# A hybrid diffusion block on one core: r feature-major, s and the output projection in 512-column pieces

## Chip, core and metric

The kernel runs on one core of one Trainium2 chip. The metric is the device time of one execution in microseconds (us). TensorE (PE) multiplies, with its weight load (PEld) beside it; VectorE (DVE), ScalarE (ACT) and GpSimd (POOL) do the element work; SyncE (SP) issues most transfers from a queue in order. The chip grants TensorE one of two clock levels, 1.2 or 2.4 GHz; 1.00 in the profile is the higher one.

## The reference

One layer over 1024 tokens of width 1024, with 256 context tokens, all in fp32. What matters here is the token mixer:

```python
z_a, q, k, v, r, lr_f, lr_b, gates = split_cols(h @ w_in)      # one input projection; z_a = (u, s)
y_a = spatial_gating(gelu(z_a), ...) @ w_a                     # u * (128x128 mixing of layer_norm(s))
o   = gla forward + gla backward                               # gated linear attention, 4 heads, both directions
o_n = o * rsqrt(mean(o * o) + EPS) * gla_g                     # per head
y_b = (o_n * silu(r)) @ w_b
x   = x + gt1 * ((g_a * y_a + g_b * y_b) @ w_out)
```

After it the x is normalised again, a router picks two of sixteen experts for each token, and the experts' feed-forward is added. The kernel spends the second half of its time on the experts, which the change does not touch.

## The kernel before

Every fp32 matrix is split in two parts, a high part rounded to the type that TensorE multiplies fast (`wh`, `hxh`) and the rest (`wl`, `hxl`). A product is three matmuls: high by high, high by low, low by high (`gemm`, L251 to L256). A contraction over 1024 has 8 steps of 128, so a gemm of one tile is 24 matmuls. A weight chunk of 1 MB is loaded by SP (`wraw`, two buffers), rounded by ScalarE (L236, 128x2048) and subtracted by VectorE (L237); `wh` and `wl` have two buffers each. The normalised input stays on the chip with features on the partitions (`H`).

The stages, in order of time: v and the low-rank gates; k and q; **r** (268 to 360 us); the GLA over the context (to 413 us) and over the tokens, first half (to 543 us) and second half (to 688 us); **s** (to 779 us); position mixing with ga (to 870 us); the projections w_a and w_b (to 1036 us); the **output projection** with residual, norm and router (to 1150 us); the experts.

- r (L583 to L594): four chunks of 256 output columns. For each of eight token tiles the tokens are stationary and the 256 weight columns move. ScalarE applies silu out of PSUM (L593), SP stores to `r_d`, token by token. k (L573 to L581) has it the other way: 128 weight columns stationary, 512 tokens moving, one full PSUM bank.
- GLA (L776 to L808): eight pairs of blocks of 128 tokens, one forward and one backward. From the fifth pair on a block has been seen by the other direction: `op` (the other direction's output) and `rb` (its rows of r) are loaded, VectorE adds, normalises by head and multiplies by r (L801, four instructions). After each pair come two side tiles, 48 matmuls each, that make gb, u or ga (`side_tile`); behind each side tile one second block is transposed on TensorE (tile `ogt`, L759), scaled by `gla_g` on ScalarE (L762, eight instructions of 128x128) and stored (`turned_out`).
- A block itself (`gla_block`): VectorE makes `ke` (L656); TensorE transposes it (`keT`); ScalarE and VectorE split it (`kt0` L661, `kt1` L662); attention, masked by VectorE (L677), split again; `o` and `s` tiles of matmuls; VectorE updates the states (L699).
- s (L823 to L830): four chunks of 256 columns, tokens stationary, as r; gelu by ScalarE (L829), statistics of 256 columns by VectorE (L830).
- Output projection (L986 to L1012, loop at L1202): w_out in four pieces of 256 columns, two in the shared buffers and two in their own. A token tile has two halves of 512 columns, each in one PSUM bank and made of two pieces. VectorE multiplies a half by gt1 (L1010) and adds x (`xt`, L1011); TensorE transposes the tile (L1023) for the router, and VectorE has its many small operations of 16 columns and fewer, for the tile before, between the two halves.

A recording layer and a scheduler write each engine's instructions in an order; each engine then runs its own list strictly in order. `issue_after` holds a piece of work in that order behind a given instruction.

Of the kernel before, what the change touches and what calls it, by code (L numbers as in the profile page):

```python
# [6 lines left out]
F32 = mybir.dt.float32  # L7
# [11 lines left out]
S = 1024  # L19
# [43 lines left out]
            + [("s", 1024 + 256 * i, 256) for i in range(4)]  # L63
# [58 lines left out]
def lay_out(x, c, ctx, c_ctx, w_mod, b_mod, g_norm1, g_norm2, w_in, w_gate2, b_gate2, gla_norm_g, sgu_ln_g,  # L122
# [28 lines left out]
    A["w_out"] = tiled(np.asarray(w_out)[0], 8, 256)  # L151
# [9 lines left out]
def body(tc, A, out):  # L161
# [15 lines left out]
    r_d = scratch((S, D), "r_d")  # L177
# [405 lines left out]
    for j in range(4):  # L583
        w = w_in("r", j)
        if j == FOLD:
            fold_router()
        if j < 2:
            mod_chunk(6 + j)
        for i in range(8):
            p = mm()  # L590
            gemm(p[:, :256], H(128 * i, 128), W_(w, 0, 256), 8)
            s = tv.tile([128, 264], F32, name="vs", bufs=3)
            silu_end = SC.activation(s[:, :256], p[:, :256], AF.Silu)  # L593
            SP.dma_start(r_d[128 * i:128 * i + 128, 256 * j:256 * j + 256], s[:, :256])  # L594
# [159 lines left out]

    def turned_out(b, ob, gt):
        for h in range(2):
# [3 lines left out]
            for k in range(4):  # L760
                c = 4 * h + k
                SC.activation(gt[:, 128 * c:128 * c + 128], p[:, 128 * k:128 * k + 128], AF.Copy,  # L762
                              scale=cols[:, C_GLA + c:C_GLA + c + 1])
        SP.dma_start(gT_d[b], gt)

    seen = set()
    for i in range(8):
        for d in range(2):
# [10 lines left out]
            if second:  # L779
                op = t1.tile([128, D], F32, name="op", bufs=2)  # L780
                SP.dma_start(op, o_d[t0:t0 + 128])
                rb = t1.tile([128, D], F32, name="rb", bufs=1)
                SP.dma_start(rb, r_d[t0:t0 + 128])
# [15 lines left out]
            for h in range(4):  # L799
                hs = slice(256 * h, 256 * h + 256)  # L800
                V.scalar_tensor_tensor(ob[:, hs], ob[:, hs], ss[:, 4 + h:5 + h], rb[:, hs],  # L801
                                       op0=ALU.mult, op1=ALU.mult)
            late.append((b, ob, gt))
        for n in range(SIDE[i]):
# [17 lines left out]
    bst = [t1.tile([128, 4, 6], F32, name=f"bst{i}") for i in range(8)]  # L822
    for j in range(4):  # L823
        w = w_in("s", j)
        for i in range(8):
            p = mm()
            gemm(p[:, :256], H(128 * i, 128), W_(w, 0, 256), 8)
            s = vs[i][:, 256 * j:256 * j + 256]
            SC.activation(s, p[:, :256], AF.Gelu_apprx_tanh)  # L829
# [9 lines left out]
    t1.release()  # L839
    zp = tc.alloc_tile_pool(name="zp", bufs=1, side="right", reuse_waits="tile")  # L840
# [109 lines left out]
    for j in range(4):  # L950
        raw = wp.tile([128, WMAX], F32, name="wraw", tag="wraw", bufs=2)
        SP.dma_start(raw[:, :2048], A["w_out"][j])
        if j < 2:
            wo.append(split(raw, 2048, 8, wp))
        else:
            wh = t1.tile([128, 8, 256], F32R, name=f"woh{j}")
            wl = t1.tile([128, 8, 256], F32R, name=f"wol{j}")
# [754 lines left out]
```

## Time and profile before

| | us |
|---|---|
| median of 3 runs | 2205.27 |
| lowest, highest | 2201.27, 2208.33 |
| the profiled execution's own time | 2202.61 |
| its span in the profile | 2200.9 |
| TensorE busy | 2146.6 (98%) |
| VectorE busy | 1413.5 (64%) |
| ScalarE busy | 1054.0 (48%) |

The span is what the records cover; 1.7 us of the execution's time lie around it. A stage's window shows how long the stage takes and how much of it each engine is busy; the timeline gives start, duration, engine and line of each instruction, and in brackets how long its engine had been idle and for what.

### The profile page before, as it was taken

Reading aid. Unit: us, or ns where it says so; the run is one execution under the profiler, and the core shown is the slowest. Engines: PE = TensorE matmul, PEld = TensorE weight load, DVE = VectorE, ACT = ScalarE, POOL = GpSimd, SP = SyncE. Lnnn points to the kernel's source line nnn. Section 1 sums busy time; section 2 is a strip of 40 time slices with the busy share of each in tenths; the row PEclk is TensorE's granted clock in tenths of the full one; section 3 lists DMA queues with packets and bytes.
Section 4 is the critical chain, followed back from the end, with each engine's and each line's share of the span. In section 5 each row is a group of like instructions: output and inputs, shape, how many; then the busy total and the mean of one; then the engine's idle time right before and its main releaser. Section 6 shows DMA issues by size and latency. Waiting matters only on the chain. (4 is left out here: it accounts for less than half of the span.)

```text
span 2200.9 us, 36059 instructions
## 1 busy us (share of the span) xinstructions
PE 2146.6 (98%) x14288; PEld 1786.6 (81%) x14289; DVE 1413.5 (64%) x2123; ACT 1054.0 (48%) x1327; POOL 201.7 (9%) x172
## 2 busy tenths in 40 slices
PE   8999999999999999999996999999999999999996
PEld 6999898888889987888995777787878777777774
DVE  5654213856763244435788778787878787786766
ACT  3412113644543134323225566676757666665653
POOL 0011000000000000000231301010101010101021
PEclk9999999999999999999997999999999999999998
DMA  7576443465662155644566989798989889897764
GB/s 301 178 221 178 158 145 112 163 201 182 204 232 80 46 205 198 219 151 147 183 248 225 340 298 369 305 371 298 378 305 352 327 325 349 303 366 289 278 235 171
DMA packets 142031, 530.20 MB, mean 241 GB/s; under 512 B 17210, under 2 KB 57842, under 8 KB 94752
## 3 DMA queue, kind: packets, MB, share of 16 engines
q1 hardware_dynamic: 119920, 468.03, 57.8%
q0 software_dynamic: 20784, 55.54, 8.6%
q10 hardware_dynamic: 1152, 4.26, 0.6%
q8 instruction: 114, 1.87, 0.3%
q14 instruction: 61, 0.50, 0.1%
HBM read 457.55 MB, written 70.31 MB: 240 GB/s over the span
## 5 line engine op out<-in xcount | busy, mean ns | idle before, releaser
L1192 DVE TENSOR_TENSOR hl<-praw,hl 128x2048 fp32r<-128x2048 f32 x173 | 395.8, 2291 | 119.9 <-ACT hl L1191 114.5
L1372 PE MATMUL pa<-hl,xah 128*128 128x512 f32 x1536 | 418.7, 394 | 2.0 <-DVE hl L1192 1.0
L1191 ACT ACTIVATE hl<-praw 128x2048 fp32r<-128x2048 f32 x173 | 331.9, 1919 | 146.5 <-PE pa L1372 146.5
L1372 PEld LDWEIGHTS pa<-hl,xah 128*128 128x128 f32 x1536 | 285.9, 189 | 65.6 <-DVE hl L1192 4.3
L1192 DVE TENSOR_TENSOR hl<-raw,hl 128x2048 fp32r<-128x2048 f32 x115 | 263.1, 2291 | 86.3 <-ACT hl L1191 82.5
L1191 ACT ACTIVATE hl<-raw 128x2048 fp32r<-128x2048 f32 x115 | 220.7, 1919 | 105.2 <-PE pa L1372 100.4
L1372 PE MATMUL pa<-hl,xal 128*128 128x512 f32 x768 | 237.3, 390 | 0.0
L255 PE MATMUL mm<-wh,hxh 128*128 128x256 f32 (+1 forms) x768 | 219.3, 286 | 0.7 <-DVE ctx_v L284 0.4
L255 PE MATMUL mm<-wl,hxh 128*128 128x256 f32 (+1 forms) x768 | 218.0, 284 | 0.0
L255 PE MATMUL mm<-wh,hxl 128*128 128x256 f32 (+1 forms) x768 | 217.7, 284 | 0.0
L1372 PE MATMUL pa<-hl,aah 128*128 128x512 f32 x768 | 211.7, 397 | 0.0
L255 PE MATMUL mm<-hxh,wh 128*128 128x512 f32 x448 | 176.7, 394 | 0.0
L255 PE MATMUL mm<-hxh,wl 128*128 128x512 f32 x448 | 176.5, 394 | 0.0
L255 PE MATMUL mm<-hxl,wh 128*128 128x512 f32 x448 | 176.5, 394 | 0.0
L1372 PEld LDWEIGHTS pa<-hl,xal 128*128 128x128 f32 x768 | 144.6, 188 | 30.8
L1372 PEld LDWEIGHTS pa<-hl,aah 128*128 128x128 f32 x768 | 142.1, 189 | 28.2 <-issue 0.4
L255 PEld LDWEIGHTS mm<-wh,hxh 128*128 128x128 f32 x768 | 146.7, 191 | 1.5 <-DVE ctx_v L284 0.6
L255 PEld LDWEIGHTS mm<-wl,hxh 128*128 128x128 f32 x768 | 146.8, 191 | 0.0
L255 PEld LDWEIGHTS mm<-wh,hxl 128*128 128x128 f32 x768 | 146.5, 191 | 0.0
L237 DVE TENSOR_TENSOR wl<-wraw,wh 128x2048 fp32r<-128x2048 f32 (+1 forms) x36 | 82.7, 2298 | 99.0 <-ACT wh L236 78.3
L1372 PE MATMUL pa<-hl,aal 128*128 128x512 f32 x384 | 120.0, 392 | 0.0
L236 ACT ACTIVATE wh<-wraw 128x2048 fp32r<-128x2048 f32 (+1 forms) x36 | 69.0, 1918 | 65.0 <-PE mm L255 64.9
(496 smaller groups left out, 3576.0 us busy)
## 6 DMA issues: line engine op xcount, KB each, us to landing
praw<-in_w_gu_dram SPq DMA_DIRECT2D x114, 1024.0 KB
raw<-in_w_gu_dram SPq DMA_DIRECT2D x78, 1024.0 KB
praw<-in_w_d_dram SPq DMA_DIRECT2D x59, 1024.0 KB
raw<-in_w_d_dram SPq DMA_DIRECT2D x37, 1024.0 KB
wraw<-in_w_in_dram SPq DMA_DIRECT2D x24, 1024.0 KB
wraw<-in_w_mod_dram SPq DMA_DIRECT2D x18, 1024.0 KB
vb<-v_d POOLq DMA_DIRECT2D x16, 1024.0 KB, 6.7
xt<-in_x_dram SPq DMA_DIRECT2D x16, 512.0 KB
```

Of the source, the lines that this page charges most:

```text
L236: SC.activation(wh[:, :n], raw[:, :n], AF.Copy)
L237: V.tensor_sub(wl[:, :n], raw[:, :n], wh[:, :n].bitcast(F32))
L255: end = PE.matmul(acc, Wst[a](k), Wmv[b](k), start=n == 0, stop=n == tot - 1)
L1191: SC.activation(hl[:, 0, :], raw, AF.Copy)
L1192: V.tensor_sub(hl[:, 1, :], raw, hl[:, 0, :].bitcast(F32))
L1372: end = PE.matmul(acc[h], st[x][:, k0 + k, :], w[:, k, 512 * h:512 * h + 512], start=start and (k, n) == (0, 0), stop=stop and (k, n) == ( ...
```

## The change

1. r becomes feature-major: 128 weight columns stationary, 512 tokens moving, 16 tiles in place of 32, and `r_d` has features first.
2. So r can be multiplied only after the transposition. The four multiplies of L801 become four scaled copies on ScalarE, without r, and `turned_out` has VectorE multiply the transposed PSUM tile by `gla_g` and by `rb` in one instruction (eight of 128x128). `rb` has one buffer, is fetched by `gate_b` for the first waiting block, and for the next one as soon as `turned_out` is through with this one.
3. s has two chunks of 512 columns. A chunk's weights are two halves of the contraction (4 steps each). The first chunk's lie in the common `wh`/`wl` buffers, the second's in a new pool `ws` of four tiles.
4. w_out is laid out as four pieces of 512 columns and half the contraction; a tile's half is 24 matmuls of 512 columns in place of 48 of 256.
5. The x rows of a token tile are fetched one tile ahead.

```diff
--- before.py
+++ after.py
@@ -60,7 +60,7 @@
             + [("r", 4096 + 256 * i, 256) for i in range(4)]
             + [("gb", 6176 + 256 * i, 256) for i in range(4)]
             + [("u", 256 * i, 256) for i in range(4)]
-            + [("s", 1024 + 256 * i, 256) for i in range(4)]
+            + [("s", 1024 + 512 * i, 512) for i in range(2)]
             + [("ga", 5152 + 256 * i, 256) for i in range(4)])
 
 
@@ -148,7 +148,7 @@
     A["sgu_w"] = f(np.asarray(sgu_w)[0].transpose(2, 0, 1))
     A["w_a"] = tiled(np.asarray(w_branch_a)[0], 8, 256)
     A["w_b"] = tiled(np.asarray(w_branch_b)[0], 8, 256)
-    A["w_out"] = tiled(np.asarray(w_out)[0], 8, 256)
+    A["w_out"] = f(np.asarray(w_out)[0].reshape(2, 4, 128, 2, 512).transpose(3, 0, 2, 1, 4).reshape(4, 128, 2048))
     A["w_router"] = f(np.asarray(w_router).reshape(8, 128, 16).transpose(1, 0, 2))
     wg, wu, wd = (np.asarray(w)[0] for w in (w_exp_gate, w_exp_up, w_exp_down))
     wgu = np.stack([w.reshape(E, 4, 2, 128, 3, 4, 128) for w in (wg, wu)], 6)
@@ -174,7 +174,7 @@
     u_d = scratch((128, 8, S), "u_d")
     ma_d = scratch((128, 8, S), "ma_d")
     ga_d = scratch((128, 8, S), "ga_d")
-    r_d = scratch((S, D), "r_d")
+    r_d = scratch((128, 8, S), "r_d")
     gbl_d = scratch((128, 8, S), "gbl_d")
     o_d = scratch((S, D), "o_d")
     gT_d = scratch((8, 128, D), "gT_d")
@@ -586,12 +586,13 @@
             fold_router()
         if j < 2:
             mod_chunk(6 + j)
-        for i in range(8):
-            p = mm()
-            gemm(p[:, :256], H(128 * i, 128), W_(w, 0, 256), 8)
-            s = tv.tile([128, 264], F32, name="vs", bufs=3)
-            silu_end = SC.activation(s[:, :256], p[:, :256], AF.Silu)
-            SP.dma_start(r_d[128 * i:128 * i + 128, 256 * j:256 * j + 256], s[:, :256])
+        for cc in range(2):
+            for t0 in (0, 512):
+                p = mm()
+                gemm(p, W_(w, 128 * cc, 128), H(t0, 512), 8)
+                s = t1.tile([128, 512], F32, name="ks", bufs=3)
+                silu_end = SC.activation(s, p, AF.Silu)
+                SP.dma_start(r_d[:, 2 * j + cc, t0:t0 + 512], s)
     t1.release()
     tv.release()
     xp.release()
@@ -752,6 +753,13 @@
         V.memset(at[d], 0.0)
     late = []
 
+    rb = None
+
+    def gate_b(b):
+        nonlocal rb
+        rb = t1.tile([128, 8, 128], F32, name="rb", bufs=1)
+        SP.dma_start(rb, r_d[:, :, 128 * b:128 * b + 128])
+
     def turned_out(b, ob, gt):
         for h in range(2):
             p = ax("ogt")
@@ -759,9 +767,11 @@
                 PE.transpose(p[:, 128 * k:128 * k + 128], ob[:, 512 * h + 128 * k:512 * h + 128 * k + 128], ident)
             for k in range(4):
                 c = 4 * h + k
-                SC.activation(gt[:, 128 * c:128 * c + 128], p[:, 128 * k:128 * k + 128], AF.Copy,
-                              scale=cols[:, C_GLA + c:C_GLA + c + 1])
+                V.scalar_tensor_tensor(gt[:, 128 * c:128 * c + 128], p[:, 128 * k:128 * k + 128],
+                                       cols[:, C_GLA + c:C_GLA + c + 1], rb[:, c, :], op0=ALU.mult, op1=ALU.mult)
         SP.dma_start(gT_d[b], gt)
+        if late:
+            gate_b(late[0][0])
 
     seen = set()
     for i in range(8):
@@ -779,8 +789,6 @@
             if second:
                 op = t1.tile([128, D], F32, name="op", bufs=2)
                 SP.dma_start(op, o_d[t0:t0 + 128])
-                rb = t1.tile([128, D], F32, name="rb", bufs=1)
-                SP.dma_start(rb, r_d[t0:t0 + 128])
             po = gla_block(d, CT + t0, kb, vb, qb, t1, at[d], mk[:, d])
             ahead(i // 2 + 1, i % 2, d)
             ob = t1.tile([128, D], F32, name="ob", bufs=2)
@@ -798,9 +806,10 @@
             rstd(ss[:, 4:8], ss[:, 0:4], 4, 1.0 / 256, t1)
             for h in range(4):
                 hs = slice(256 * h, 256 * h + 256)
-                V.scalar_tensor_tensor(ob[:, hs], ob[:, hs], ss[:, 4 + h:5 + h], rb[:, hs],
-                                       op0=ALU.mult, op1=ALU.mult)
+                SC.activation(ob[:, hs], ob[:, hs], AF.Copy, scale=ss[:, 4 + h:5 + h])
             late.append((b, ob, gt))
+            if len(late) == 1:
+                gate_b(b)
         for n in range(SIDE[i]):
             side_tile(*todo.pop(0))
             if late:
@@ -819,14 +828,29 @@
 
     t1 = tc.alloc_tile_pool(name="t1", bufs=1, reuse_waits="tile")
     vs = [t1.tile([128, D], F32, name=f"vs{i}") for i in range(8)]
-    bst = [t1.tile([128, 4, 6], F32, name=f"bst{i}") for i in range(8)]
-    for j in range(4):
-        w = w_in("s", j)
+    bst = [t1.tile([128, 2, 6], F32, name=f"bst{i}") for i in range(8)]
+    ws = tc.alloc_tile_pool(name="ws", bufs=1, side="right", reuse_waits="tile")
+    for j in range(2):
+        w = [[], []]
+        for kh in range(2):
+            o, n = off["s"][j]
+            src = A["w_in"][:, o + 4 * n * kh:o + 4 * n * (kh + 1)]
+            if j == 0:
+                parts = wload(src, 2048, 4)
+            else:
+                raw = wp.tile([128, WMAX], F32, name="wraw", tag="wraw", bufs=2)[:, :2048]
+                SP.dma_start(raw, src)
+                wh, wl = (ws.tile([128, 2048], F32R, name="wide", bufs=4) for x in range(2))
+                SC.activation(wh, raw, AF.Copy)
+                V.tensor_sub(wl, raw, wh.bitcast(F32))
+                parts = [a.rearrange("p (k n) -> p k n", k=4) for a in (wh, wl)]
+            for x in range(2):
+                w[x].append(parts[x])
         for i in range(8):
             p = mm()
-            gemm(p[:, :256], H(128 * i, 128), W_(w, 0, 256), 8)
-            s = vs[i][:, 256 * j:256 * j + 256]
-            SC.activation(s, p[:, :256], AF.Gelu_apprx_tanh)
+            gemm(p, H(128 * i, 128), tuple(lambda k, a=a: a[k // 4][:, k % 4, :] for a in w), 8)
+            s = vs[i][:, 512 * j:512 * j + 512]
+            SC.activation(s, p, AF.Gelu_apprx_tanh)
             V.bn_stats(bst[i][:, j, :], s)
     mv = t1.tile([128, 8, 2], F32, name="mv")
     lr_ = t1.tile([128, 8], F32, name="lr_")
@@ -837,6 +861,7 @@
         V.tensor_scalar(vs[i], vs[i], mv[:, i, 0:1], lr_[:, i:i + 1], op0=ALU.subtract, op1=ALU.mult)
         SP.dma_start(vh_d[128 * i:128 * i + 128], vs[i])
     t1.release()
+    ws.release()
     zp = tc.alloc_tile_pool(name="zp", bufs=1, side="right", reuse_waits="tile")
     t2 = tc.alloc_tile_pool(name="t2", bufs=1, side="right", reuse_waits="tile")
 
@@ -951,11 +976,11 @@
         raw = wp.tile([128, WMAX], F32, name="wraw", tag="wraw", bufs=2)
         SP.dma_start(raw[:, :2048], A["w_out"][j])
         if j < 2:
-            wo.append(split(raw, 2048, 8, wp))
+            wo.append(split(raw, 2048, 4, wp))
         else:
-            wh = t1.tile([128, 8, 256], F32R, name=f"woh{j}")
-            wl = t1.tile([128, 8, 256], F32R, name=f"wol{j}")
-            rv = raw[:, :2048].rearrange("p (k n) -> p k n", k=8)
+            wh = t1.tile([128, 4, 512], F32R, name=f"woh{j}")
+            wl = t1.tile([128, 4, 512], F32R, name=f"wol{j}")
+            rv = raw[:, :2048].rearrange("p (k n) -> p k n", k=4)
             SC.activation(wh, rv, AF.Copy)
             V.tensor_sub(wl, rv, wh.bitcast(F32))
             wo.append((wh, wl))
@@ -986,16 +1011,21 @@
     def out_gemm(i, p, pieces):
 
         for n in pieces:
-            q, k0 = n // 2, 4 * (n % 2)
-            w = wo[q]
-            for k in range(k0, k0 + 4):
+            h, k0 = n // 4, 2 * (n % 4)
+            w = wo[2 * h + k0 // 4]
+            for k in range(k0, k0 + 2):
                 for a, b in ((0, 0), (0, 1), (1, 0)):
-                    PE.matmul(p[q // 2][:, 256 * (q % 2):256 * (q % 2) + 256], mT[i // 4][a][:, i % 4, k, :], w[b][:, k, :],
+                    PE.matmul(p[h], mT[i // 4][a][:, i % 4, k, :], w[b][:, k % 4, :],
                               start=(k, a, b) == (0, 0, 0), stop=(k, a) == (7, 1))
 
+    xts = {}
+
+    def fetch_x(i):
+        xts[i] = t1.tile([128, D], F32, name="xt", bufs=2)
+        SP.dma_start(xts[i], A["x"][128 * i:128 * i + 128])
+
     def fetch(i):
-        xt = t1.tile([128, D], F32, name="xt", bufs=2)
-        SP.dma_start(xt, A["x"][128 * i:128 * i + 128])
+        xt = xts.pop(i)
         x1 = t1.tile([128, D], F32, name="x1", bufs=2)
         xa = t1.tile([128, D], F32, name="xa", bufs=1)
         h2 = t1.tile([128, 4, QW], F32, name="h2", bufs=2)
@@ -1199,8 +1229,11 @@
         pages.pop(0)
         return tuple(hl[:, j, :].rearrange("p (k n) -> p k n", k=2) for j in range(2))
 
+    fetch_x(0)
     for i in range(8):
         fetch(i)
+        if i < 7:
+            fetch_x(i + 1)
         p = [mm(), mm()]
         out_gemm(i, p, PC[0])
         if i == 4:
```

How the order of instructions moves, at two places on VectorE. First the border between the seventh and the eighth pair of blocks, second-half GLA. Before (`ob` is a block's output, `ke`, `kt1`, `at0`, `ats1` belong to the next block, `wl` is a chunk of side-tile weights):

```order
L801 SCALAR_TENSOR_TENSOR ob_6369<-ob_6369,ss_6370,rb_6290 128x256 x4
L656 TENSOR_TENSOR ke_6684<-la_5574,cf_6681 128x256
L656 TENSOR_TENSOR ke_6684<-la_5976,cf_6681 128x256
L237 TENSOR_TENSOR wl_6965<-wraw_6962,wh_6964 128x2048
L662 TENSOR_TENSOR kt1_6581<-keT_6575,kt0_6580 128x512
L677 COPY_PREDICATED at0_4120<-mk_4118,att_6587 64x4x64 x2
L699 SCALAR_TENSOR_TENSOR S00_3751<-S00_3751,cf_6567,s_6621 128x256
L680 TENSOR_TENSOR ats1_6600<-at0_4120,ats0_6599 128x512
```

After (line numbers are the changed kernel's; `op` at L770 is the transposed block, `ogt` the PSUM tile):

```order
L222 SCALAR_TENSOR_TENSOR ss_5920<-rs_t_5930,rs_y_5929 128x4
L770 SCALAR_TENSOR_TENSOR op_5726<-ogt_6008,cols_79,rb_5832 128x128 x4
L770 SCALAR_TENSOR_TENSOR op_5726<-ogt_6017,cols_79,rb_5832 128x128 x4
L770 SCALAR_TENSOR_TENSOR op_5840<-ogt_6085,cols_79,rb_6027 128x128 x4
L770 SCALAR_TENSOR_TENSOR op_5840<-ogt_6094,cols_79,rb_6027 128x128 x4
L663 TENSOR_TENSOR kt1_6131<-keT_6125,kt0_6130 128x512
L678 COPY_PREDICATED at0_3672<-mk_3670,att_6137 64x4x64 x2
L657 TENSOR_TENSOR ke_6234<-la_5124,cf_6231 128x256
L700 SCALAR_TENSOR_TENSOR S00_3303<-S00_3303,cf_6117,s_6171 128x256
L681 TENSOR_TENSOR ats1_6150<-at0_3672,ats0_6149 128x512
```

The multiplies by r stood ahead of the transposition; now the eight behind it stand ahead of `kt1`, and the weight subtraction L237 has moved behind the next block's attention, the second of its two `ke` too.

Second, the end of the GLA and the start of s. Before, the subtraction that follows the last multiply by r belongs to the second s chunk:

```order
L222 SCALAR_TENSOR_TENSOR ss_6754<-rs_t_6764,rs_y_6763 128x4
L801 SCALAR_TENSOR_TENSOR ob_6753<-ob_6753,ss_6754,rb_6674 128x256 x4
L237 TENSOR_TENSOR wl_7187<-wraw_7184,wh_7186 128x2048
L830 BN_STATS bst0_6954<-vs0_6946 128x6
L830 BN_STATS bst1_6955<-vs1_6947 128x6
```

After, `wide` belongs to the second s chunk, and `wl_6526` to the second half of the contraction of the first s chunk:

```order
L770 SCALAR_TENSOR_TENSOR op_6110<-ogt_6401,cols_79,rb_6216 128x128 x2
L845 TENSOR_TENSOR wide_6754<-wraw_6751,wide_6753 128x2048
L770 SCALAR_TENSOR_TENSOR op_6224<-ogt_6469,cols_79,rb_6411 128x128 x4
L770 SCALAR_TENSOR_TENSOR op_6224<-ogt_6478,cols_79,rb_6411 128x128 x4
L237 TENSOR_TENSOR wl_6526<-wraw_6523,wh_6525 128x2048
L854 BN_STATS bst0_6506<-vs0_6498 128x6
```

The first s chunk's second half of weights now stands behind the last block's transposed multiplies.

## Rows read from the trace of the kernel before

**Rows 1.** The page: span, and busy time of each engine.
```profile
span 2200.9 us, 36059 instructions
PE 2146.6 (98%) x14288; PEld 1786.6 (81%) x14289; DVE 1413.5 (64%) x2123; ACT 1054.0 (48%) x1327; POOL 201.7 (9%) x172
```

**Rows 2.** Windows: the r, GLA second half, s and output stages.
```profile
core 0: us, PE busy (x) PEld busy (x) DVE busy (x) ACT busy (x) POOL busy (x), PEclk, DMA share, GB/s
268.50:360.40 91.90, 91.90 (x773) 91.57 (x772) 14.49 (x19) 17.31 (x34) 2.19 (x4) 1.00 0.40 135
543.00:688.00 145.00, 144.21 (x854) 122.20 (x853) 96.42 (x266) 73.87 (x206) 3.18 (x6) 1.00 0.58 192
688.00:779.00 91.00, 91.00 (x750) 90.56 (x750) 23.36 (x49) 20.75 (x37) 0.00 (x0) 1.00 0.16 53
1036.00:1150.00 114.00, 112.14 (x997) 109.17 (x995) 90.90 (x354) 31.10 (x65) 32.61 (x36) 1.00 0.62 209
```

**Rows 3.** Timeline of ScalarE: evictions in k, r, s; brackets: wait.
```profile
223.44 0.60 ACT L580 ACTIVATE ks<-mm 128x512 f32<-128x512 f32 x1 [4.84 <-PE mm L255]
...
301.25 0.38 ACT L593 ACTIVATE vs<-mm 128x256 f32<-128x256 f32 x1 [2.50 <-PE mm L255]
...
742.13 0.38 ACT L829 ACTIVATE vs<-mm 128x256 f32<-128x256 f32 x1 [2.50 <-PE mm L255]
```

**Rows 4.** Timelines of VectorE and TensorE, output projection: a steady tile.
```profile
1102.55 0.69 DVE L1010 TENSOR_TENSOR x<-mm,gt 128x512 f32<-128x512 f32 x1
...
1106.61 0.17 DVE L1071 TENSOR_TENSOR R<-R 128x8 f32<-128x8 f32 x1 [0.38 <-ACT R L1067]
...
1112.14 0.59 DVE L1028 TENSOR_TENSOR ss<-ss 128x1 f32<-128x1 f32 x1 [0.79 <-ACT h L1012]
...
1116.48 0.68 DVE L1010 TENSOR_TENSOR x<-mm,gt 128x512 f32<-128x512 f32 x1
...
1111.91 0.27 PE L1023 MATMUL x1t<-kf,x 128*128 128x128 f32 x1
...
1125.62 0.27 PE L1023 MATMUL x1t<-kf,x 128*128 128x128 f32 x1
```

**Rows 5.** Output stage: VectorE's groups, and a residual of tile 0 (timeline).
```profile
L1011 DVE TENSOR_TENSOR x<-x,xt 128x512 f32<-128x512 f32 x16 | 11.1, 692 | 0.2
...
1056.64 0.69 DVE L1010 TENSOR_TENSOR x<-mm,gt 128x512 f32<-128x512 f32 x1 [2.52 <-PE mm L993]
```

**Rows 6.** Timelines of VectorE and ScalarE at a border between pairs.
```profile
639.43 0.17 DVE L222 SCALAR_TENSOR_TENSOR ss<-rs_t,rs_y 128x4 f32<-128x4 f32 x1
...
639.63 1.67 DVE L801 SCALAR_TENSOR_TENSOR ob<-ob,ss,rb 128x256 f32<-128x256 f32 x4
...
648.36 0.76 DVE L656 TENSOR_TENSOR ke<-la,cf 128x256 f32<-128x256 f32 x2 [7.06 <-PE keT L659]
...
649.04 2.28 DVE L237 TENSOR_TENSOR wl<-wraw,wh 128x2048 fp32r<-128x2048 f32 x1
...
651.80 0.69 DVE L662 TENSOR_TENSOR kt<-keT,kt 128x512 fp32r<-128x512 f32 x1 [0.48 <-ACT kt L661]
...
649.11 2.17 ACT L762 ACTIVATE op<-ogt,cols 128x128 f32<-128x128 f32 x8
```

**Rows 7.** Timelines: kb's issue and first use; two transposes (ogt) of a pair.
```profile
631.79 0.53 SPq L774 DMA_DIRECT2D kb<-kT_d  x1
...
638.29 0.43 DVE L655 TENSOR_TENSOR la<-la,kb 128x256 f32<-128x256 f32 x1 [3.69 <-DMA kb<-kT_d]
...
635.06 0.27 PE L759 MATMUL ogt<-kf,ob 128*128 128x128 f32 x1
...
646.85 0.27 PE L759 MATMUL ogt<-kf,ob 128*128 128x128 f32 x1
```

**Rows 8.** Timelines of ScalarE and VectorE: the last split before s.
```profile
683.43 1.91 ACT L236 ACTIVATE wh<-wraw 128x2048 fp32r<-128x2048 f32 x1 [4.47 <-PE mm L255]
...
685.37 2.29 DVE L237 TENSOR_TENSOR wl<-wraw,wh 128x2048 fp32r<-128x2048 f32 x1 [11.96 <-ACT wh L236]
```

## The prediction

> **What bounds the kernel now.** I read the page first. TensorE is busy for 2146.6 of 2200.9 us, so what TensorE does not have to do is the first place to look [rows 1]. The windows by stage come next: in the stage that makes r TensorE is busy for all of its 91.90 us, in the s stage for all of its 91.00, in the second half of the GLA for 144.21 of 145.00, in the output projection for 112.14 of 114.00. The granted clock is 1.00, the 2.4 GHz level, in all four, so the clock is nothing to win or lose here [rows 2]. But a busy engine is not yet the one that sets the pace, so I read who is waited for, tile by tile. In the r stage the ScalarE eviction takes 0.38 us and then waits 2.50 us for TensorE: a period of 2.88 us, set by TensorE. In the s stage it is the same row with the same numbers. In the k stage, which already uses 512 columns, one eviction of 0.60 us follows a wait of 4.84: a period of 5.44 us for 24 matmuls of 512 columns [rows 3]. The output projection reads differently, and that decides a third of the forecast (below).
>
> **r and s.** Before, a tile is 24 matmuls of 256 columns in 2.88 us, 0.120 us each; a 512-column one costs 5.44 / 24 = 0.227 us, which is 0.1133 for each 256 columns [rows 3]. r has 32 tiles before, 32 x 2.88 = 92.2 us, and 16 after, 16 x 5.44 = 87.0: **-5.1 us**. s has the same counts: **-5.1 us**. That r changes its orientation (weights stationary, tokens moving) makes it exactly the k stage's form. The evictions halve in number and grow to 0.60 us, hidden under 5.44; the DMA share of the r stage is 0.40 and the bytes stay [rows 2], so nothing there can become late. The BN statistics on 512 columns are not in the trace; between the eviction rows they have 5.44 us, and hide.
>
> The Trainium skill (TensorE: Matmul & The Clock Gate, section Back-to-back issue gap) gives the spacing as N / 2.4 ns plus 2.5 ns. By it a stage would go from 768 x 109.2 ns to 384 x 215.8 ns, an estimate of -1.0 us where I take -5.1; the rows say 0.120 and 0.227 us, some 11 ns above that formula for either width, and the measurement decides.
>
> **The output projection.** Its 768 matmuls shrink by the same 5.1 us, or 0.64 per token tile. But VectorE's first residual multiply of a tile (L1010) stands at 1102.55 and at 1116.48, a period of 13.93, and between the two VectorE waits twice, 0.38 and 0.79 us, both times for ScalarE and never for TensorE. TensorE's own work has a shorter period: its transposes of x1 (L1023) stand at 1111.91 and 1125.62, 13.71 apart [rows 4]. VectorE's chain of small router operations carries the stage, and the change touches none of it. So TensorE gets faster behind an engine that does not. Where VectorE does wait for matmuls is the start, 2.52 us in tile 0 [rows 5]. I take one tile's share, **-0.7 us**. Bounds: 0 (VectorE alone carries it) and -5.1 (it follows TensorE in full).
>
> **GLA, second half.** Per block VectorE loses four multiplies by r (L801, 1.67 us) and ScalarE gets four scaled copies of 128x256 in their place; ScalarE loses eight scaled 128x128 copies out of PSUM (2.17 us) and VectorE gets eight scalar_tensor_tensor of that size [rows 6]. That form is not in the trace: from below 0.2 us each (the step of the 128x4 operation L222 to the next), from above 0.42 (L801, four in 1.67) [rows 6]; I take the middle, 0.3, so 2.4 us for eight. VectorE gains about 0.7 us of work a block in a stage where it is busy 96 of 145 us [rows 2].
>
> What matters is where it stands. The first two order pieces show VectorE at the border between two pairs of blocks. In the trace its idle 7.06 us, which end with the keT transposes, are followed by ke, the weight subtraction L237 (2.28 us) and then kt1 (651.80), which ScalarE's eight L762 copies had held up by its kt0 [rows 6]. After, the eight multiplies of the second transposed block stand ahead of kt1, and L237 behind it. A new 2.4 us replaces 0.76 + 2.28 us, and ScalarE's eight copies are gone from in front of kt0. That is near even. The o tiles need a PSUM bank which these multiplies set free, and TensorE has fewer filler matmuls there, so I charge **+1.0 us** for the three borders between pairs (the fourth is the start of s, below). Bounds: -0.8 (all that TensorE now idles in this stage [rows 2]) and 7 (three borders at 2.4 us).
>
> The second matter is the r block. It now has one buffer that is fetched only after the multiplies of the block before. The nearest row is the kb load, 128 partitions and 512-byte pieces like it: issued 631.79, used 638.29, so 6.5 us [rows 7] for 256 KB; r has 512 KB, so 6.5 to 8 us. The two transposes of one pair stand at 635.06 and 646.85, 11.8 apart [rows 7]; less some 3 us until the first block's multiplies are done, 8.8 remain. It fits, with less than 2.5 us to spare.
>
> **The start of s.** Before, the subtraction at 685.37 prepares the second s chunk and is not needed for 23 us [rows 8]. After (the last order piece) VectorE has the last block's eight multiplies (2.4), then L237 (2.28) for the second k-half of the *first* chunk. Its buffer comes free only when the last ga matmul is done. TensorE meanwhile has the second transpose group (0.5) and 12 or 13 matmuls of the first k-half (13 x 0.227 = 2.9). 2.4 + 2.3 - 0.5 - 2.9 = 1.3, with the hand-overs **+1.5 us**. Bounds: 0 and 4.6 (nothing hides it). ScalarE's half of this split, 1.91 us [rows 8], stands beside it.
>
> **The early x rows** are worth 0: no row of VectorE in the output projection waits for x in [rows 4, 5].
>
> **Sum.** -5.1 - 5.1 - 0.7 + 1.0 + 1.5 = -8.4 us. The profiled execution took 2202.61, which makes 2194.2; the median of the runs is 2205.27, 2.7 higher, and from there it is 2196.9. I forecast **2196 us**. A measurement of this kernel tells 0.3%, 6.6 us, from no change: below 2198.7 is faster, above 2211.9 slower.
>
> **Rivals.**
> 1. *The output projection follows TensorE* after all, since VectorE's order has slack that I do not see (it is busy 90.90 of 114 us [rows 2]): -5.1 in place of -0.7, 2192. Against it: VectorE waits for nothing of TensorE's in a steady tile [rows 4]. 0.13.
> 2. *The losses eat the gain.* The borders cost 4 in all (some half of their upper bound) and the s start 3.5: -5.1 - 5.1 - 0.7 + 4 + 3.5 = -3.4, 2202, within 0.3%. For it: TensorE has only 0.8 us of idle time in the second half of the GLA [rows 2], so any lateness there shows in full. Against it: VectorE has 7.06 us without work just ahead of a border [rows 6]. 0.20.
> 3. *Slower: the single r buffer.* r's load comes after the transposes at all second blocks of a pair; VectorE stands in order before that multiply, so kt1, the masked copies and the state updates of the next GLA block stand behind it, and TensorE runs out of matmuls. Without the GLA term the sum is -9.4, so it decides from +16 on, four late loads of 4 us each: with the 8.8 us of room that is a load of 12.8 us, twice the kb row [rows 7]. For it: DMA is 0.58 busy there, a 1 MB weight load may share the queue [rows 2]. At 5 us each 2205.27 - 9.4 + 20 = 2216. 0.10.
> 4. *Long matmuls gain nothing in r and s*: what a short matmul costs beyond its columns would not be a cost of the instruction, and two halves of 512 columns would keep the pace of two matmuls of 256. Then -0.7 + 1.0 + 1.5 = +1.8, 2207. The k stage's 5.44 us speaks against it [rows 3]. 0.03. (The skill's formula named above, -1.0 a stage, would give 2206.)
>
> The forecast's own case has 0.54, range 2191 to 2201: some 0.45 of it below 2198.7. With rival 1: faster 0.58; same 0.32 (rivals 2 and 4 and 0.09 of the forecast's); slower 0.10. The range reaches to rival 1 with its spread below and past rival 2 above: 2187 to 2208.
>
> **What would show it.** Right: r evictions 5.44 us apart, both stages near 87 us; a wait of 1 to 2 us by TensorE for wl (L237) a dozen matmuls into s; the L1010 period still 13.9 with TensorE now waiting for x1 at L1023. Wrong: an L1010 period near 13.1 (rival 1), waits of TensorE for kt1 or the PSUM bank of several us at each border (rival 2), VectorE waiting for the DMA of rb at L770 (rival 3), or tiles of r further apart than 5.5 us.

## The result and the profile after

The changed kernel takes 2191.25 us (median of 5 runs, 2188.57 to 2195.82) against 2205.27 before: a ratio of 0.9945, 95% interval 0.9929 to 0.9960, or 12 us (9 to 16) saved; the two medians by themselves are 14.0 apart. A second timing beside other kernels gave 0.9954 (0.9942 to 0.9967), 10 us (7 to 13). The forecast was 2196 and a gain of 8.4 us.

The profiled execution took 2195.82 us, its span is 2194.1: it is the slowest of the five, and saves only 6.8 us of span. So the first thing to find out is which stage of it is not typical. The page's first two lines:

```profile
span 2194.1 us, 33656 instructions
PE 2134.7 (97%) x13136; PEld 1725.3 (79%) x13137; DVE 1414.6 (64%) x2139; ACT 1045.9 (48%) x1263; POOL 201.9 (9%) x172
```

TensorE has 12 us less to do than in [rows 1]. The windows of the four stages, which answer to [rows 2] (r, GLA second half, s, output projection):

```profile
core 0: us, PE busy (x) PEld busy (x) DVE busy (x) ACT busy (x) POOL busy (x), PEclk, DMA share, GB/s
271.00:361.30 90.30, 90.30 (x413) 74.66 (x412) 15.94 (x20) 16.82 (x21) 2.20 (x4) 1.00 0.38 135
540.00:681.00 141.00, 140.89 (x831) 119.47 (x831) 100.68 (x293) 73.32 (x175) 3.17 (x6) 1.00 0.65 209
681.50:771.00 89.50, 88.45 (x392) 72.96 (x391) 20.76 (x34) 16.25 (x21) 0.00 (x0) 1.00 0.14 48
1034.60:1142.00 107.40, 104.42 (x593) 84.75 (x592) 88.66 (x343) 29.57 (x63) 30.39 (x33) 1.00 0.62 202
```

TensorE is still full in r and in the GLA, has a gap of 1 us in s, and now 3 us of gaps in the output projection, 1.2 of which, for `wl` at its start, stood there before too. Where the time went is best read from fixed points of the work, taken from the timelines: the last eviction of k, the last group of eight `ogt` transpositions, the last eviction of s, the first and the last matmul of the output projection, the experts' first transposition, each by its start. The stretches between them, in us:

| stretch | before | after | after, 2nd profile | r alone (e1) | r 256 wide (e7) | s alone (e2) | w_out alone (e3) | e5 | e12 |
|---|---|---|---|---|---|---|---|---|---|
| start to the end of k | 266.93 | 270.41 | 269.05 | 266.70 | 266.72 | 266.57 | 269.18 | 267.30 | 266.74 |
| r and GLA | 416.53 | 410.31 | 410.39 | 410.32 | 415.28 | 416.35 | 415.52 | 410.35 | 410.42 |
| s | 93.23 | 89.47 | 89.47 | 93.23 | 93.22 | 88.72 | 93.22 | 88.13 | 88.12 |
| mixing, w_a, w_b | 263.32 | 264.47 | 265.08 | 265.03 | 263.43 | 265.20 | 262.96 | 264.25 | 263.84 |
| output projection | 108.58 | 107.06 | 106.95 | 108.58 | 108.65 | 108.83 | 108.04 | 106.57 | 104.64 |
| router, to the experts | 25.44 | 25.71 | 25.87 | 25.01 | 25.63 | 24.86 | 25.68 | 25.80 | 21.16 |
| experts | 1026.87 | 1026.67 | 1025.89 | 1027.43 | 1025.37 | 1026.67 | 1026.30 | 1025.80 | 1025.98 |

Behind the end of k the change saves 10.3 us; ahead of it this execution loses 3.5, in work that the change does not touch. The timeline shows where: TensorE waits for VectorE's `vv`, which waits for ScalarE, whose `vv` buffers wait for the stores of v; and the granted clock is below full speed in the windows around it.

```profile
144.78 0.48 PE L255 MATMUL mm<-wh,hxh 128*128 128x264 f32 x1 [2.27 <-DVE vv L284]
```
```profile
138.00:142.00 4.00, 4.00 (x36) 4.00 (x35) 0.43 (x1) 0.25 (x1) 0.69 (x1) 1.00 0.86 270
142.00:146.00 4.00, 1.73 (x11) 1.51 (x10) 0.86 (x2) 0.78 (x2) 0.89 (x2) 0.87 0.04 10
146.00:150.00 4.00, 4.00 (x26) 4.00 (x26) 0.49 (x2) 0.78 (x2) 1.16 (x2) 0.71 0.53 135
```

A wait of 2.27 us and, behind it, a window at a mean clock of 0.71, part of it at the lower of the two levels: 3.5 us together.

The evictions of r (L594) and s (L853) answer to [rows 3], as forecast, 0.60 + 4.84 = 5.44 us apart:

```profile
308.38 0.60 ACT L594 ACTIVATE ks<-mm 128x512 f32<-128x512 f32 x1 [4.84 <-PE mm L255]
...
742.99 0.60 ACT L853 ACTIVATE vs<-mm 128x512 f32<-128x512 f32 x1 [4.84 <-PE mm L255]
```

At the start of s VectorE runs the last eight multiplies, then the split; TensorE does 13 matmuls and waits. Timeline of VectorE, then of TensorE (answers to [rows 8]):

```profile
681.35 2.16 DVE L770 SCALAR_TENSOR_TENSOR op<-ogt,cols,rb 128x128 f32<-128x128 f32 x8 [3.12 <-PE ogt L767]
683.43 2.28 DVE L237 TENSOR_TENSOR wl<-wraw,wh 128x2048 fp32r<-128x2048 f32 x1
...
685.77 0.50 PE L255 MATMUL mm<-wl,hxh 128*128 128x512 f32 x1 [1.05 <-DVE wl L237]
```

At the border between the seventh and the eighth pair (VectorE, answers to [rows 6]):

```profile
644.97 2.16 DVE L770 SCALAR_TENSOR_TENSOR op<-ogt,cols,rb 128x128 f32<-128x128 f32 x8 [9.63 <-PE ogt L767]
647.22 0.69 DVE L663 TENSOR_TENSOR kt<-keT,kt 128x512 fp32r<-128x512 f32 x1
```

The multiplies take 2.16 us, and start when the transposition is done, not when r has landed: in both profiles of the changed kernel VectorE's idle time ahead of L770 ends with `ogt` alone. kt1 starts right behind them, 2.88 us after the transposition began at 644.34; before, it was 4.95 (646.85 to 651.80 [rows 6, 7]). Most of the 0.8 us that TensorE idled in the second half of the GLA before was one wait of an `o` tile for ScalarE's eight copies (L762) to free a PSUM buffer; after, there is no such wait. The waits of TensorE before:

```profile
PE o L685 <- ACT op L762: 0.7, 1, 0.7
```

A steady tile of the output projection (VectorE, and TensorE's wait for x1; answers to [rows 4]):

```profile
1096.24 0.68 DVE L1040 TENSOR_TENSOR x<-mm,gt 128x512 f32<-128x512 f32 x1
...
1110.25 0.68 DVE L1040 TENSOR_TENSOR x<-mm,gt 128x512 f32<-128x512 f32 x1
...
1105.25 0.30 PE L1053 MATMUL x1t<-kf,x 128*128 128x128 f32 x1 [0.58 <-DVE x L1041]
```

VectorE's period is 14.01, as long as before, and TensorE waits at the transpose. It does so from the fifth tile on. In the tiles before, its transposes are 13.1 to 13.3 apart, where [rows 4] had 13.71 (TensorE, after):

```profile
1064.32 1.03 PE L1053 MATMUL x1t<-kf,x 128*128 128x128 f32 x8
...
1077.54 1.03 PE L1053 MATMUL x1t<-kf,x 128*128 128x128 f32 x8
```

In the kernel before TensorE had no wait in the stage but 1.2 us for `wl` at its start. So TensorE set the pace there, and VectorE fell behind by 0.2 us a tile; now TensorE is 0.5 us a tile faster until VectorE's lag stops it.

### The profile page after: what moved, and what is told of

It is laid out like the page before. It is cut to its first block, busy times and chain, and to the rows that moved or that the text cites. A ratio compares the mean times of both kernels' runs of the same rounds, so it can differ in the third digit from the quotient of the medians.

```text
span 2194.1 us, 33656 instructions
## 1 busy us (share of the span) xinstructions
PE 2134.7 (97%) x13136; PEld 1725.3 (79%) x13137; DVE 1414.6 (64%) x2139; ACT 1045.9 (48%) x1263; POOL 201.9 (9%) x172
## 5 line engine op out<-in xcount | busy, mean ns | idle before, releaser
L255 PE MATMUL mm<-hxh,wh 128*128 128x512 f32 x576 | 226.8, 394 | 0.0
L255 PE MATMUL mm<-hxh,wl 128*128 128x512 f32 x576 | 226.7, 393 | 0.0
L255 PE MATMUL mm<-hxl,wh 128*128 128x512 f32 x576 | 225.4, 391 | 0.0
L237 DVE TENSOR_TENSOR wl<-wraw,wh 128x2048 fp32r<-128x2048 f32 (+1 forms) x34 | 78.1, 2297 | 88.0 <-ACT wh L236 87.9
L255 PEld LDWEIGHTS mm<-hxh,wl 128*128 128x128 f32 x576 | 108.3, 188 | 21.3 <-issue 0.4
L255 PEld LDWEIGHTS mm<-hxl,wh 128*128 128x128 f32 x576 | 108.3, 188 | 20.9
L255 PEld LDWEIGHTS mm<-hxh,wh 128*128 128x128 f32 x576 | 108.3, 188 | 20.6 <-issue 0.4
L255 PE MATMUL mm<-wh,hxh 128*128 128x264 f32 (+1 forms) x320 | 99.1, 310 | 2.6 <-DVE vv L284 2.3
L255 PE MATMUL mm<-wl,hxh 128*128 128x264 f32 (+1 forms) x320 | 98.3, 307 | 1.1 <-DVE wl L237 1.1
L255 PE MATMUL mm<-wh,hxl 128*128 128x264 f32 (+1 forms) x320 | 98.1, 307 | 0.0
```

Of the source, the lines that this page charges most:

```text
L237: V.tensor_sub(wl[:, :n], raw[:, :n], wh[:, :n].bitcast(F32))
L255: end = PE.matmul(acc, Wst[a](k), Wmv[b](k), start=n == 0, stop=n == tot - 1)
```

## The experiments

Times are ratios to the kernel before, measured beside it on one chip, 95% interval in brackets; us are worked out from its median there (2202.5 to 2205.5).

**The parts one by one (e1 to e4).** Each is the diff's own hunks, put into the kernel before: r with the multiply behind the transposition, s, or w_out alone (none of them has the early x rows); e4 is the changed kernel again.

e1, r alone:

> The kernel before with r feature-major alone (and the multiply by r behind the transposition that it needs). Theory (the matmul pace, 16 x 5.44 in place of 32 x 2.88, with the GLA even or a little better): 4 to 7 us faster than before, TensorE waiting under 1 us between the end of r and the start of s. Rival (the border between pairs and the single r buffer cost what was feared): under 2 us faster or slower, with waits of TensorE for kt or for a PSUM bank, and of VectorE for the DMA of rb.

0.9972 (0.9961 to 0.9983): 6.2 us faster. r and GLA are 6.2 us shorter, with 0.6 us of TensorE waits in the GLA; the rival falls.

e2, s alone:

> The kernel before with s in 512-column chunks alone. Theory: 5.1 us less matmul time, less the wait for the second half of the first chunk's weights (about 1 us here, since VectorE has no transposed multiplies in front of it), less some 1 us that position mixing waits longer for its loads: 3 to 4 us faster. Rival (the loads that position mixing waits for set its end, so an earlier end of s buys nothing): 0 to 1 us faster, with 3 us or more of TensorE waits in the mixing.

0.9982 (0.9973 to 0.9991): 4.0 us faster. The s stage is 4.5 shorter, mixing to w_b 1.9 longer; the wait for the first chunk's second half is 0.3 us (see e5), not the 1 expected. The rival falls. Whether part of its mechanism is there stays open: TensorE's waits in the mixing are 4.3 us against 2.5 before, but e1, where s is as before, has 3.9.

e3, w_out alone:

> The kernel before with w_out in 512-column pieces alone. Theory (VectorE's chain carries the stage): 0.5 to 2 us faster, the period of the first residual multiply stays at 13.9 us and TensorE waits for x1 at the transposes. Rival (the stage follows TensorE): 4 to 6 us faster, period near 13.1 us.

1.0004 (0.9995 to 1.0014): nothing, not even the 0.5 us expected, though the profile has the stage 0.5 us shorter (and a wait in the v stage, below). VectorE's residuals keep their period of 13.97, and TensorE waits for x1. Timeline, then the waits of TensorE in the stage (total, times, longest):

```profile
1088.45 0.68 DVE L1010 TENSOR_TENSOR x<-mm,gt 128x512 f32<-128x512 f32 x1
...
1102.42 0.68 DVE L1010 TENSOR_TENSOR x<-mm,gt 128x512 f32<-128x512 f32 x1
```
```profile
PE x1t L1023 <- DVE x L1011: 2.7, 3, 1.7
PE mm L993 <- DVE wl L237: 1.2, 1, 1.2
```

1.7 of the 2.7 us belong to one tile with a period of 15.12, in which VectorE itself waits for the x rows (timeline):

```profile
1118.31 0.69 DVE L1011 TENSOR_TENSOR x<-x,xt 128x512 f32<-128x512 f32 x1 [1.25 <-DMA xt<-in_x_dram]
```

Neither profile of the changed kernel, which fetches x a tile ahead, has that wait, and its stage is 1.0 us shorter than e3's. So the early x rows look worth about 1 us once TensorE is faster; no run has them alone.

The parts sum to 9.3 us; the whole, which has the early x rows too, is 10.1 in the same timing: they add up within the intervals.

e4, the changed kernel again:

> The changed kernel once more, unaltered, for a second profiled execution. Theory (the 2.3 us wait and the lower clock in the v stage of the first profile belong to that one execution, a late store): no such wait here, and a span 3 to 4 us below the first one's 2194.1, so near 2190. Rival (the change brings that wait): it stands here too, at 130 to 150 us.

0.9954 (0.9942 to 0.9967). My expectation failed: the wait stands in this profile too, 2.1 us. Counting all profiled executions, TensorE waits 1.48 us or longer for `vv` in eight of ten with the new w_out layout (not in e5 and e12, which have it) and in none of the four without it (before, e1, e2, e7). That is no proof, since the layout changes nothing before 1030 us except the order of the bytes in one input. Whether the wait belongs to the change or to the execution stays open.

**Width or orientation (e7).** On e1:

```diff
-            for t0 in (0, 512):
+            for t0 in (0, 256, 512, 768):
                 p = mm()
-                gemm(p, W_(w, 128 * cc, 128), H(t0, 512), 8)
+                gemm(p[:, :256], W_(w, 128 * cc, 128), H(t0, 256), 8)
```

(The eviction and the store behind it take 256 columns as well.)

> The kernel before with r feature-major, as in the kernel with r alone, but its matmuls 256 tokens wide: 768 of them, 32 evictions. Theory (r's gain is the width: 0.120 against 0.227 us for twice the columns, and the GLA gains 1 to 1.5 us beside it): 1 to 2 us faster than the kernel before, 4 to 5 slower than with 512, r evictions 2.88 us apart. Rival (the orientation or the GLA's new form carries the gain): 4 us or more faster than before, evictions closer than 2.8 us.

0.9989 (0.9980 to 0.9998): 2.4 us faster, so 3.8 of e1's 6.2 are the width, and in the profile 5.0 (the stretch of r and GLA: 415.28 against 410.32). The evictions are 2.88 apart:

```profile
303.92 0.39 ACT L594 ACTIVATE ks<-mm 128x256 f32<-128x256 f32 x1 [2.50 <-PE mm L255]
```

The remaining 1.2 us of the stretch (416.53 against 415.28) are what the new orientation and the new form of the GLA give by themselves; 0.7 of them is the wait for ScalarE's copies shown above, which e7 does not have.

**The wait at the start of s (e5).** On the changed kernel:

```diff
-            if j == 0:
+            if kh == 0:
                 parts = wload(src, 2048, 4)
```

> The changed kernel with the weights of s exchanged between the pools: the first half of the contraction of both s chunks in the common buffers, the second half of both in the pool ws, so that the first chunk's second half is split during the GLA. Theory (the 1.05 us wait after 13 matmuls is the buffer of the last ga chunk and VectorE's order): that wait goes, the s stage is 1.0 us shorter, 83 to 84 us less its start, the whole 0 to 1 us faster than the changed kernel. Rival (the transposed multiplies on VectorE are what is late): a wait of 1 us stays, on another weight tile.

0.9945 (0.9930 to 0.9960), 12 us faster than before: 0 to 2 us ahead of the changed kernel's two ratios, which the intervals cannot tell apart. The profile can: no wait in the s stage, which takes 88.13 in place of 89.47, a little more than the wait of 1.05. So the wait came of a split that had to stand behind the last ga chunk, and the rival as it was put, a wait on another weight tile, falls. But the transposed multiplies have their share in it: in e2, with the same buffers and without them, TensorE waits 0.3 us at the same place (waits of TensorE, e2):

```profile
PE mm L255 <- DVE wl L237: 0.3, 1, 0.3
```

**The single r buffer (e8).** On the changed kernel, ahead of rb's load:

```diff
+        rj = t1.tile([128, 6, 128], F32, name="rj", bufs=1)
+        SP.dma_start(rj, r_d[:, 0:6, 128 * b:128 * b + 128])
         SP.dma_start(rb, r_d[:, :, 128 * b:128 * b + 128])
```

> The changed kernel with a second load of 384 KB of r, into a tile that nobody reads, issued just ahead of each load of rb, so that rb lands later by some three quarters of its own time. Theory (the room at the second block of a pair is 8.8 us and rb needs 6.5 to 8): VectorE now waits for the DMA of rb at the multiplies, 2 to 5 us at four places, TensorE loses 0 to 3 us at each, 0 to 8 us slower than the changed kernel. Rival (rb has far more room than that): no such wait, same time.

0.9977 (0.9965 to 0.9989), 5 to 7 us slower than the changed kernel, but not by the theory. Nobody reads the extra tile, so the scheduler put seven of its eight loads at 413 to 443 us on SP's queue, 155 us and more ahead of the loads of rb that they were to delay, among the loads of the GLA's first half; there the q block came late (VectorE's timeline), TensorE waited 4.8 us, and r and GLA are 6.4 us longer. SP's queue, then VectorE:

```profile
412.78 0.38 SPq L762 DMA_DIRECT2D rj<-r_d  x1
```
```profile
429.08 0.69 DVE L667 TENSOR_TENSOR qq<-ep,qb 128x512 f32<-128x512 f32 x1 [3.02 <-DMA qb<-qT_d]
```

It does not test rb's room, which stays unmeasured beyond this: it was enough in every profile.

**Who carries the output projection (e6, e9 to e12).** e6, on the changed kernel, the second norm of all tiles as the last tile has it:

```diff
-            if last:
+            if True:
                 hs = slice(512 * h, 512 * h + 512)
                 scaled = SC.activation(xa[:, hs], xa[:, hs], AF.Copy, scale=ss[:, 3:4])
                 end = GP.tensor_add(h2[:, 2 * h:2 * h + 2, 0:256], xa[:, hs].rearrange("p (a b) -> p a b", a=2),
                 ...
```

> The changed kernel with the second norm of every token tile (L1041 of before, two operations, 1.42 us a tile on VectorE) as a scaled copy on ScalarE and an addition on GpSimd. Theory (VectorE's chain carries the output projection and hides what 512 columns save): the period of the first residual multiply falls from 13.97 to 12.6 to 13.3 us, until TensorE carries it at about 13.07 (13.71 less 0.64), and the stage becomes 4 to 6 us shorter. Rival (the period is set by a loop of latencies through ScalarE and TensorE, not by VectorE's work): period stays at 13.9, the stage as long as it was.

0.9997 (0.9988 to 1.0007): all of the gain lost, the stage 117.97 us. Both theories missed: the period rose. TensorE waits for the hT copies, which stand behind the new copies in ScalarE's queue (waits of TensorE):

```profile
PE lgt L1079 <- ACT hT L1054: 6.9, 4, 2.6
```

That is about half of the 10.9 us. For the rest TensorE is busier, 109.4 us in the stage in place of 104.1: behind the two longest waits the granted clock is 0.54 to 0.81 in windows of 4 us, where the changed kernel has 1.00. What the additions on GpSimd did here was not separated.

e9, on e5, the work left out and put nowhere:

```diff
-            V.scalar_tensor_tensor(h2[:, 2 * h:2 * h + 2, 0:256], a2v(xa), ss[:, 3:4], a2v(sh2), op0=ALU.mult,
-                                   op1=ALU.add)
+            V.scalar_tensor_tensor(h2[:, 2 * h:2 * h + 2, 0:16], a2v(xa)[:, :, 0:16], ss[:, 3:4], a2v(sh2)[:, :, 0:16],
+                                   op0=ALU.mult, op1=ALU.add)
```

> The kernel with the weights of s exchanged (e5), with the two second-norm operations of VectorE cut to 16 of each 256 columns for the first seven token tiles; the experts' inputs h2 of these tokens are therefore mostly not computed. Nothing is put on another engine. Theory (VectorE's work carries the output projection): each period of the first residual multiply falls from 13.97 by about 1.1 (two operations of 0.75 become 0.2) towards TensorE's 13.07, the stage becomes 4 to 6 us shorter. Rival (a loop of latencies from engine to engine sets the period): under 0.3 us a tile, the stage stays at 106.5.

0.9927 (0.9902 to 0.9952): 4 us ahead of e5, though the intervals overlap. The period falls to 12.6 to 13.9, the stage to 104.66, 1.9 us less (the end of the span gains 2.8 more, among experts that read other inputs). So VectorE does hold the stage up, though less than the expected 4 to 6 us was to be had: TensorE's transposes are 13.2 us apart here, with no wait in the stage but the 1.2 us at its start, so TensorE sets the rest. One period (timeline):

```profile
1062.71 0.68 DVE L1040 TENSOR_TENSOR x<-mm,gt 128x512 f32<-128x512 f32 x1
...
1075.46 0.69 DVE L1040 TENSOR_TENSOR x<-mm,gt 128x512 f32<-128x512 f32 x1
```

e10 and e11, on e5, one or both operations of VectorE to GpSimd, which is idle there for 9 of 14 us (the edit is e11's; e10 has it for the second half of a tile alone):

```diff
-            V.scalar_tensor_tensor(h2[:, 2 * h:2 * h + 2, 0:256], a2v(xa), ss[:, 3:4], a2v(sh2), op0=ALU.mult,
-                                   op1=ALU.add)
+            GP.tensor_scalar(a2v(xa), a2v(xa), ss[:, 3:4], None, op0=ALU.mult)
+            GP.tensor_add(h2[:, 2 * h:2 * h + 2, 0:256], a2v(xa), a2v(sh2))
```

> The kernel e5 with one of the two second-norm operations a tile moved from VectorE to GpSimd (a scaling and an addition, 2.6 us there by its 1.3 us operations of this size). Theory (VectorE's work carries the stage, GpSimd is free): period 13.2 to 13.4, stage 3 to 4 us shorter. Rival (latency loop, or GpSimd's operations slow VectorE's): no shorter stage.

> The kernel e5 with both second-norm operations a tile moved from VectorE to GpSimd (four operations, 5.2 us a tile beside its 2.6 us of multiplies, of 13 us). ScalarE's order stays as it is, unlike with the copies on ScalarE, which queued in front of the hT copies. Theory (VectorE's work carries the stage): period about 13.1, stage 4 to 6 us shorter, the whole 3 to 6 us faster than e5. Rival (latency loop, or GpSimd slows VectorE): no shorter stage, same time or slower.

0.9963 (0.9951 to 0.9976) and 0.9994 (0.9982 to 1.0005): 4 and 11 us slower than e5 by the ratios (e10's interval overlaps e5's), with the stage 3.7 and 9.6 us longer in the profiles, and periods of 14.0 to 15.0 and 14.7 to 16.6. The more GpSimd does, the longer VectorE takes. (In e11 the granted clock also fell, to 0.50 in the window of 1097 to 1101 us.) Timelines of e11, VectorE and GpSimd:

```profile
1105.01 1.15 DVE L1107 TENSOR_TENSOR R<-R 128x4 f32<-128x4 f32 x1
...
1104.82 1.32 POOL L1044 TENSOR_TENSOR xa<-x,a 128x512 f32<-128x512 f32 x1
```

An operation of 4 columns, which takes 0.16 elsewhere, takes 1.15 and ends at 1106.16; GpSimd's ends at 1106.14. With that in mind the trace of the kernel before shows the same thing, and I had read over it:

```profile
1104.43 1.25 DVE L1123 SCALAR_TENSOR_TENSOR R<-R 128x16 f32<-128x16 f32 x1
...
1104.36 1.29 POOL L1014 TENSOR_TENSOR xa<-x,a 128x512 f32<-128x512 f32 x1
```

The Trainium skill (SBUF — State Buffer, section SBUF: two separate sides) says that VectorE and GpSimd have one pair of SBUF ports in common, held for a whole instruction, and that a VectorE operation with two SBUF inputs blocks fully behind a GpSimd operation that reads SBUF. These rows agree: 1.25 us in place of 0.17, with the same end.

e12, on e5, GpSimd's multiplication `xa` on VectorE:

```diff
-XAP = True
+XAP = False
```

> The kernel e5 with the multiplication xa (two of 128x512 a token tile, 1.3 us each on GpSimd) on VectorE. ScalarE's order stays. Theory (while GpSimd runs such a multiplication, a VectorE operation with two tensors in SBUF stands still until it ends: one of 128x16 at 1104.43 takes 1.25 us in place of 0.17 and ends with GpSimd's at 1105.65, and L1028 takes 0.60): the two stretched operations fall to 0.17, which gives back 1.5 us a tile, the two new ones cost 1.4: period 13.7 to 14.0 as with GpSimd, stage 105 to 108 us, the whole within 2 us of e5. Rival (the stretching is something else): period 15.3, stage 10 us longer, the whole 8 to 10 us slower than e5.

0.9901 (0.9885 to 0.9918): **22 us faster than before, 10 faster than e5** by the ratios, 7.3 by the spans of the profiles (2182.73 us, the best kernel of this study). The mechanism held, its size was too small: I had counted the stretched operations and the new ones, not that the second new one (0.69) fills a time in which VectorE stood idle. In e5 it waits 0.79 us for ScalarE ahead of L1058, as in [rows 4]; here it waits under 0.1. VectorE has 1.4 us more work a tile and is done sooner; the period is 13.2 here and 12.6 to 13.3 in other tiles but one (15.1). TensorE carries the stage, with transposes 13.2 us apart in every tile and no wait but the 1.2 us at the start, and the router behind it is 4.6 us shorter, for a reason that I did not trace. Timeline of VectorE in e12:

```profile
1074.43 0.69 DVE L1040 TENSOR_TENSOR x<-mm,gt 128x512 f32<-128x512 f32 x1 [0.15 <-PE mm L1018]
...
1076.71 0.17 DVE L1153 SCALAR_TENSOR_TENSOR R<-R 128x16 f32<-128x16 f32 x1
...
1087.65 0.69 DVE L1040 TENSOR_TENSOR x<-mm,gt 128x512 f32<-128x512 f32 x1 [0.15 <-PE mm L1018]
```

VectorE now waits for TensorE (0.15), which it never did in a steady tile of the kernel before.

## Why the prediction was right, and where it was not

The direction, the range and the mechanism held; of the five terms three were near, one was half of what came, and one had the wrong sign.

- **r and s, -5.1 each.** Right in kind: the tiles are 5.44 us apart, and e7 shows for r that the width does it: 5.0 in the profile, 3.8 by the ratios. The s stage, without its first wait (e5), is 5.1 us shorter. The Trainium skill's formula that the prediction quotes is, in the section named there, that of a matmul by itself; for a stream of weight loads and matmuls, which these stages are, the section gives other figures, so it was no forecast of them.
- **Start of s, +1.5.** 1.05 us, after 13 matmuls, for the weight tile named. The net -3.6 of the stage measured -3.8.
- **Output projection, -0.7.** e3 has no gain by its ratio and 0.5 us by its profile; in the whole the stage lost 1.5. Rival 1 falls: VectorE's period stayed at 14.0. But "VectorE's chain of small router operations carries the stage" was half a reading: VectorE's period was the longer one, and yet TensorE, which waited for nothing in a steady tile, set the pace, so the tiles up to the fifth gained and not one tile's share. The full worth of the halved matmuls in this stage is the 3.9 us of e12. The early x rows, put at 0, seem to be worth about 1 us of it (e3). What I called a chain of small operations was in part VectorE standing still behind GpSimd; the change could not win there, e12 could.
- **GLA, +1.0.** This step failed: "I charge +1.0 us for the three borders". The new form gains 1.2 us (e7). The eight multiplies cost 2.16 (I took 2.4), but with ScalarE's eight copies gone kt1 comes 2.1 us earlier behind the transposition, and TensorE's idle time in the second half fell from 0.8 to 0.1 us: the PSUM bank for which I charged was waited for before, behind those copies, and not after. Where the other 0.5 us comes from is open. I had written that it was near even and then charged for the unknown. Rivals 2 and 3 fall with it; rival 3's point of decision was not tested (e8).
- **Not in the sum.** Mixing to w_b is 1.1 to 1.8 us longer. TensorE's waits in the mixing, before and then after:

```profile
PE mix L871 <- DVE z L873: 1.6, 2, 1.1
PE mix L871 <- DMA vg<-vh_d: 0.9, 3, 0.4
```
```profile
PE mix L896 <- DMA vg<-vh_d: 2.2, 3, 1.3
PE mix L896 <- DVE z L898: 1.5, 2, 0.9
```

  The waits for the loads of the normalised rows of s grew, but that the shorter s stage is the cause is not shown: e1, with s as before, is 1.7 us longer here too. And the wait in the v stage, 1.5 to 2.6 us, with a start up to 3.9 us longer, stands in most profiles of the changed layout, unexplained.

So -6.2 for r and GLA (forecast -4.1), -3.8 for s (forecast -3.6), +1.1 for mixing to w_b, -1.5 for the output projection and +0.1 for the rest make -10.3 without the v stage's wait, beside the two timings' -12 and -10. The forecast erred by 2.1 in r and the GLA, 0.2 in s and 0.8 in the output, less the mixing's 1.1; that the errors partly cancel is luck.

## What to carry to other kernels

Before counting a gain in matmuls, take the period of a steady tile on every engine: where another engine's is longer, the gain stops as soon as that engine's lag holds TensorE up (here from the fifth tile on; e3, 768 matmuls halved: nothing measured). Then ask why that engine's period is long; a small operation that takes seven times its usual duration is not work, and the engine that ends at the same moment is the cause. Moving work to an idle engine helps only if it shares neither queue nor ports with the busy one: to ScalarE and GpSimd it cost 11 us here, to GpSimd alone 4 and 11, and taking work away from the idle engine won 7 to 10.

## What the hardware did that I had not expected

- A VectorE operation of 128x4 or 128x16 stands still while GpSimd runs a 128x512 multiplication: 1.15 to 1.29 us in place of 0.16 to 0.22, both ending within 0.04 us (all such pairs in before and after). Over the output stage L1153 averages 0.725 us with GpSimd multiplying and 0.168 without (groups by line, after and e12):

```profile
L1153 DVE SCALAR_TENSOR_TENSOR R<-R 128x16 f32<-128x16 f32 x12 | 8.7, 725 | 0.2
```
```profile
L1153 DVE SCALAR_TENSOR_TENSOR R<-R 128x16 f32<-128x16 f32 x14 | 2.4, 168 | 0.0
```

- A wait of TensorE of 2.27 us was followed by a window at a mean clock of 0.71, in which matmuls of 264 columns start 0.22 us apart in place of 0.12 (the lower level, 1.2 GHz), and cost 3.5 us in all; in e3 a wait of 2.4 us at the same place, with the clock at 1.00 over the stretch, cost 2.3.
- Eight scalar_tensor_tensor of 128x128 with one input in PSUM take 2.16 us on VectorE, 0.26 each from start to start.
